# Hybrid decoder step on one core: the sums of w2's quarters made in SBUF and stored, or made in DRAM by copying and accumulating transfers

## The chip, the cores and the metric

The kernel runs on one core of a Trainium2 chip. The metric is the device time of one execution in microseconds (us), of which the median of several runs is taken. The engines are PE (matrix products; PEld is its weight load), DVE (vector), ACT (activations), POOL (general) and SP (which here only issues transfers). Transfers issued from SP, ACT and POOL go through three queues, which the profile calls q1 (SP), q10 (ACT) and q0 (POOL), to the same 16 DMA engines.

## The reference

The program computes one step of a one-layer decoder. 2048 prompt tokens and 8 x 8 sample tokens of width 1024 go through a common input projection. One half of the heads does forgetting attention (8 heads of 64, for the samples over 8192 cached positions), the other half an mLSTM recurrence. Then come the output projection, a layer norm, an MLP of width 4096 and a second layer norm.

```python
x1 = _layer_norm(DN_ALPHA * x + mix, ln1_g, ln1_b)
hid = jnp.square(jax.nn.relu(x1 @ w1))
return _layer_norm(DN_ALPHA * x1 + hid @ w2, ln2_g, ln2_b)
```

What matters here is `hid @ w2`. The kernel makes it by Strassen's scheme, seven products of half-sized blocks in place of eight, and for this it needs sums of w2's quarters.

## The kernel before, in words

The work runs in phases. Phase A makes the projections and the mLSTM. Phase B is the prompt's forgetting attention. Phase O makes the output projection and the first layer norm, phase C the MLP. The samples' attention over the cache is a generator whose steps are laid between the other work by a counter of estimated PE time (`tick`). In phase B that counter is set so that no step falls due; only six steps are called by hand, in units 10 to 15, each with one gather of cached keys on POOL (L1649). Every step runs inside `beside`, which holds its instructions behind the entries of the table `last` (the latest instruction of PE, ACT and DVE that the helpers have put there), each on its own engine.

**Phase B** (`phase_b`) runs over 64 units, 8 heads h by 8 groups g of 256 queries. Unit (h, g) reads 2g + 2 blocks of 128 keys, so late units of a head are longer than early ones. `scores` makes the score tiles of two blocks of 128 queries. For each of them POOL first makes `nd` (L938), the forget values `nl` of the diagonal block plus a causal mask; there are three buffers of it. PE writes q times k into a PSUM bank in two passes (L945, L946). DVE adds the forget values and keeps the maximum, for the blocks before the diagonal at L952 and for the diagonal block, with `nd`, at L956; this empties the bank for the next product. L959 makes the row's maximum. One unit later `values` takes the exponential on ACT (L973), the sums on DVE (L974), transposes the weights on PE (L986), copies them out on ACT (L989) or DVE (L991) and multiplies by v (L995). `finish`, twice per head, brings the reciprocal sums through DRAM (`drl`, L1016, L1019) and scales the output on POOL (L1021). SP loads the queries `qn` (L918), the keys `kn` (L900), and `nl` and `vn` (L894, L895).

**The sums of w2.** The host lays w2 out as 8 steps p by 4 quarters of 128 x 1024 (512 KB each). Strassen's scheme needs four sums for each step, kept in the DRAM tensor `dw2[p, j]`: j = 0 is quarters 0 + 1, j = 1 is 3 + 1, j = 2 is 0 + 1 + 3, j = 3 is 0 + 1 + 3 + 2 (each made from the one before in the same buffer). `w2_sum` is called 34 times, from unit 10 on, two calls in three units. Four calls make one step: ACT's queue loads quarters 0 and 3 into two SBUF buffers `wr` (L1094, 16 loads in all), POOL's queue adds other quarters to these buffers by accumulating transfers (L1097, 32) and stores the sums to `dw2` (L1100, 32). Each of these waits for the transfer before it on the same buffer, on the queue of the engine that issues it. POOL issues `nd` and the scaling of L1021 from the same stream of instructions, in order.

There are five `wr` buffers of 128 x 1024; phase O loads the output weights into them from unit 60 on (L1126).

**Phase C** makes the MLP in four blocks of tokens. In every block each step p loads quarters of w2 and the four sums of `dw2` by SP (L1137; 128 loads of `dw2` in all), splits them into a high and a low part (ACT at L154, DVE at L157) and makes three matmuls for each product (L162, L163, L164).

The order of instructions on each engine is laid down when the program is built, by a scheduler that simulates a timeline; `tc.issue_after(ins)` keeps an instruction behind `ins` on its engine.

Of the kernel before, what the change touches and what calls it, by code (L numbers as in the profile page):

```python
# [10 lines left out]
F32 = mybir.dt.float32  # L11
# [3 lines left out]
OP = mybir.AluOpType  # L15
# [37 lines left out]
def body(ctx, tc, I, O, stages):  # L53
    nc = tc.nc
    V, A, G, T, SY = nc.vector, nc.scalar, nc.gpsimd, nc.tensor, nc.sync
# [3 lines left out]
    drm = ctx.enter_context(tc.tile_pool(name="drm", bufs=1, space=DRAM))  # L59
# [11 lines left out]
    dR = drm.tile([NB, FH, PAST], F32, name="dR")  # L71
    dqb = drm.tile([2, NB, 32, 16 * 8], F32, name="dqb")
    dx1 = drm.tile([TOT, D], F32, name="dx1")
    dw2 = drm.tile([8, 4, 128, 1024], F32, name="dw2")

    ident = cst.tile([128, 128], F32, name="ident")
    nhalf = cst.tile([128, 8], F32, name="nhalf")
# [5 lines left out]
    def pad(pool, n):  # L83
        pads.append(n)
        V.memset(pool.tile([128, n // 4], F32, name=f"pad_{len(pads)}x")[:, 0:1], 0.0)
# [22 lines left out]
    last = {}  # L108
# [17 lines left out]
    def attend():  # L126

        r = beside(acc[1])
        if r == 3:
            acc[3] = acc[1]  # L130
        if r in (0, 3):
            acc[1] = None

    def tick(us):

        macc[0] += us
        while macc[1] and macc[0] > macc[2]:
            macc[0] -= macc[2]
            if beside(macc[1][0]) == 0:
                macc[1].pop(0)  # L140
        if not macc[1]:
            macc[0] = 0.0
        acc[0] += us
        while acc[1] is not None and acc[0] > acc[2]:
            acc[0] -= acc[2]
            attend()
# [718 lines left out]
    def phase_b():  # L865
# [8 lines left out]
        def bank():  # L874

            turn[0] += 1
            if turn[0] % 3 == 0:
                return pps.tile([128, 512], F32, name="pS", tag="sX", bufs=1)
            return ppb.tile([128, 512], F32, name="pS", bufs=2)

        def head(h):
            vn = Z[0]["vn"] if h == 0 else pb.tile([128, 16, 64], F32, name="vn", bufs=2)
            nl = pb.tile([128, 2048], F32, name="nl", bufs=2)
            if h == 0:
                masks.append(pb.tile([128, 128], F32, name="dmask"))
            ls = pb.tile([128, 32], F32, name="ls", bufs=2)
            ks = pb.tile([128, 2048], F32R, name="ks", bufs=2)
            G.memset(ls, 1.0)
            return dict(h=h, ls=ls, nl=nl, vn=vn, ks=ks)

        def forget_values(z, a, n):

            h = z["h"]
            SY.dma_start(z["nl"][:, a:a + n], dap(dnl, h * TOT + a, [[0, 128], [1, n]]))  # L894
            SY.dma_start(z["vn"][:, a // 128:(a + n) // 128], vp[a:a + n, h * 64:h * 64 + 64].rearrange("(t p) c -> p t c", p=128))  # L895
# [7 lines left out]
        def keys(z, g, kn=None):  # L903

            h = z["h"]
            kn = keys_load(h, g) if kn is None else kn
            if h == 0:
                forget_values(z, g * 512, 512)
            k = z["ks"][:, g * 512:(g + 1) * 512]
            split_hi(k, kn)  # L910
            split_lo(k[64:128], kn[64:128], k[64:128])

        def queries(z, g):

            h = z["h"]
            qn = pb.tile([128, 256], F32, name="qn", bufs=3)
            for d in range(2):
                SY.dma_start(qn[d * 64:d * 64 + 64], dq[h // 2, h % 2 * 64:h % 2 * 64 + 64, g * 256:(g + 1) * 256])  # L918
            qh = pb.tile([128, 256], F32R, name="qh", bufs=3)
            if h == 0 and g == 0:  # L920
                z["vn"] = pb.tile([128, 16, 64], F32, name="vn", bufs=2)
            ql = pb.tile([128, 256], F32R, name="ql", bufs=3)
            split_hi(qh, qn)
            split_lo(ql, qn, qh)
            z["q", g] = qh, ql

        def scores(z, g):

            qh, ql = z.pop(("q", g))
            nl, ks = z["nl"], z["ks"]  # L930
            out = []
            for i in range(2):
                qt = 2 * g + i
                n = (qt + 1) * 128
                qs = slice(i * 128, i * 128 + 128)
                mx = pb.tile([128, 8], F32, name="mx", bufs=6)
                nd = pb.tile([128, 128], F32, name="nd", bufs=3)
                G.tensor_tensor(nd, nl[:, qt * 128:n], dmask, op=OP.add)  # L938
                st = []
                j = 0  # L940
                for a in range(0, n, 512):
                    b = min(n, a + 512)
                    w = max(b - a, 256)
                    pS = bank()
                    T.matmul(pS[:, :w], qh[:, qs], ks[:, a:a + w], start=True, stop=False)  # L945
                    last["PE"] = T.matmul(pS[:, :w], ql[:, qs], ks[:, a:a + w], start=False, stop=True)  # L946
                    tick(0.42)
                    sp = pb.tile([128, 512], F32, name="S", bufs=10)
                    st.append(sp)
                    e = min(b, qt * 128)  # L950
                    if e > a:
                        last["DVE"] = V.tensor_tensor_reduce(out=sp[:, :e - a], in0=pS[:, :e - a], in1=nl[:, a:e], scale=1.0, scalar=NEG,  # L952
                                               op0=OP.add, op1=OP.max, accum_out=mx[:, j:j + 1])
                        j += 1
                    if b == n:
                        V.tensor_tensor_reduce(out=sp[:, e - a:b - a], in0=pS[:, e - a:b - a], in1=nd, scale=1.0, scalar=NEG,  # L956
                                               op0=OP.add, op1=OP.max, accum_out=mx[:, j:j + 1])
                        j += 1
                V.tensor_reduce(mx[:, 7:8], mx[:, :j], axis=AX.X, op=OP.max, negate=True)  # L959
                out.append((st, mx))  # L960
            return out
# [66 lines left out]
        kn = keys_load(0, 0)  # L1028
        queries(Z[0], 0)
        Z[0].update(head(0))  # L1030
        dmask = masks[0]
        pad(pb, 64)
        V.memset(dmask, 0.0)
        G.affine_select(dmask, dmask, pattern=[[-1, 128]], compare_op=OP.is_ge, fill=NEG, base=0, channel_multiplier=1)
        keys(Z[0], 0, kn)
        sc = {}
        LA = 1
        for n in range(len(units) + LA):
            if 10 <= n < 16 and acc[1] is not None:
                attend()  # L1040
            while len(w2_done) < 34 and n >= 10 + len(w2_done) * 3 // 2:
                w2_sum()
            if n == 60:
                wo.extend(half_wo(0, q) for q in range(4))
            if n < len(units):
                h, g = units[n]
                sc[n] = scores(Z[h], g)
                if h == 0 and g % 2 == 0 and g < 6:
                    keys(Z[0], g // 2 + 1)
                if h < 7:  # L1050
                    if g == 3:
                        Z[h + 1] = head(h + 1)
                        forget_values(Z[h + 1], 0, S)
                    if g >= 4:
                        keys(Z[h + 1], g - 4)
                if n + 1 < len(units):
                    queries(Z[units[n + 1][0]], units[n + 1][1])
            if n >= LA:
                h, g = units[n - LA]
                values(Z[h], g, sc.pop(n - LA))  # L1060
        es.close()
# [13 lines left out]
    def raw():  # L1075

        return pcw.tile([128, 1024], F32, name="wr", bufs=5)
# [2 lines left out]

        return pcw.tile([128, 1024], F32, name="xr", bufs=2)[:n]

    w2_done, w2_q = [], {}

    def w2_sum():

        k = len(w2_done)
        w2_done.append(k)

        def load(p):  # L1090
            for q in (0, 3):
                w2_q[p, q] = raw()
                with tc.issue_after(last["ACT"].ins):
                    A.dma_start(w2_q[p, q], I["w2"][p, q])  # L1094

        def add(p, a, q):
            G.dma_start(w2_q[p, a], I["w2"][p, q], accum_op=OP.add)  # L1097

        def store(p, a, j):
            G.dma_start(dw2[p, j], w2_q[p, a])  # L1100

        p, j = divmod(k, 4)
        if k == 0:
            load(0)
        if j == 0:
            if p:
                store(p - 1, 0, 2)
                add(p - 1, 0, 2)
            if p < 8:
                add(p, 0, 1)  # L1110
        elif j == 1:
            if p:
                store(p - 1, 0, 3)
            if p < 8:
                store(p, 0, 0)
                add(p, 3, 1)
        elif j == 2:
            store(p, 3, 1)
            add(p, 0, 3)
        elif p < 7:  # L1120
            load(p + 1)

    def half_wo(hf, q):

        r = raw().rearrange("p (k c) -> p k c", k=2)
        SY.dma_start(r, I["w_o2"][hf, q].rearrange("p (k c) -> p k c", k=2))  # L1126
        return r
# [800 lines left out]
```

## Time and profile before

| what | value |
|---|---|
| median of 3 runs | 3317.51 us (3309.04 to 3324.81) |
| the profiled execution's own time | 3327.42 us |
| its span | 3325.7 us |
| mean granted clock of PE | 0.976 |
| PE busy | 3155.1 us (95%) |
| DVE busy | 2106.5 us (63%) |
| ACT busy | 1504.9 us (45%) |
| POOL busy | 928.8 us (28%) |
| DMA, mean | 223 GB/s |
| phase B in the trace | about 928 to 1400 us |

The profile is one execution. A line such as L938 is the line of the kernel's code that made the instruction. An entry such as `[5.10 <-DMA wr<-w]` says that the engine stood idle for 5.10 us before the instruction and that a transfer from w2 into a `wr` buffer ended this. In the tables of stretches each engine has its busy us and, in brackets, its number of instructions; PEclk is the granted share of PE's full clock, and the DMA share is the mean busy share of the 16 DMA engines. POOL is named with the transfers that it issues, but the issue is not counted as a compute operation of the kernel; what it waits for before an issue holds all that is queued behind it on POOL.

### The profile page before, as it was taken

To read this page: it belongs to the slowest core of one execution; us is meant where nothing else is said; L and a number is where in the kernel's file an instruction comes from. 1 tells how busy PE (TensorE), PEld (TensorE's weight loads), DVE (VectorE), ACT (ScalarE), POOL (GpSimd) and SP (SyncE) were. 2 spreads that over 40 slices of the span, in tenths; PEclk is the share of its full clock that TensorE was granted. 3 is DMA by queue.
4 is the path that set the end of the run, shared out by engine and by line. 5 is a ranking of instruction groups with operands and counts; after the bars stand their busy time and mean duration, and the time that the engine had idled before them with its cause. 6 is when DMAs were issued, how large, how long until landed. Compare 5 with 4: busy or idle time off the path is not lost.

```text
span 3325.7 us, 58093 instructions
## 1 busy us (share of the span) xinstructions
PE 3155.1 (95%) x21681; PEld 2571.7 (77%) x21681; DVE 2106.5 (63%) x5079; ACT 1504.9 (45%) x2966; POOL 928.8 (28%) x977
## 2 busy tenths in 40 slices
PE   8999999998978989999999999999999999799997
PEld 8998998888945657677677777676777777698895
DVE  6857565455366868644465668656586666856658
ACT  4333343333267878722244454343454444444442
POOL 0031232332323334266533333423323121100000
PEclk9999999998988999999999999999999999999998
DMA  5575766766658777387787878878779766644333
GB/s 184 151 222 183 235 222 216 248 203 214 215 173 218 201 202 204 100 308 263 277 313 266 312 273 286 310 254 329 281 269 339 244 216 207 196 149 127 114 108 98
DMA packets 342002, 742.76 MB, mean 223 GB/s; under 512 B 63896, under 2 KB 177944, under 8 KB 340824
## 3 DMA queue, kind: packets, MB, share of 16 engines
q1 hardware_dynamic: 252856, 416.71, 39.7%
q0 software_dynamic: 83520, 304.12, 26.2%
q10 hardware_dynamic: 5344, 18.22, 1.6%
q8 instruction: 171, 2.80, 0.3%
q14 instruction: 111, 0.91, 0.1%
HBM read 669.32 MB, written 69.60 MB: 222 GB/s over the span
## 4 chain that ended last, share of the span: by engine, by line
PE 45%; DMA 4%; DVE 2%; issue 1%; POOL 1%; ACT 0%; DVEq 0%; POOLq 0%; ACTq 0%; SPq 0%
PE ph L162 8%; PE ph L163 7%; PE ph L164 7%; PE py L162 5%; PE py L164 5%; PE py L163 5%; PE sO L1784 3%; DMA vt<-cache_v,idxV 2%; PE sQ L1672 2%; DMA kT<-cache_k,idxK 1%; PE sT L1741 1%; DVE wl L157 1%; DVE y L1348 1%; DMA xr<-cache_v,idxV 0%; PE pw L163 0%
## 5 line engine op out<-in xcount | busy, mean ns | idle before, releaser
L157 DVE TENSOR_TENSOR wl<-wr,wh 128x1024 fp32r<-128x1024 f32 x364 | 445.8, 1226 | 375.8 <-ACT wh L154 372.1
L154 ACT ACTIVATE wh<-wr 128x1024 fp32r<-128x1024 f32 x364 | 382.8, 1054 | 329.3 <-PE ph L163 167.8
L162 PE MATMUL ph<-x1h,wh 128*128 128x512 f32 (+1 forms) x1280 | 455.9, 356 | 0.5 <-DVE x1l L157 0.5
L163 PE MATMUL ph<-x1l,wh 128*128 128x512 f32 (+1 forms) x1280 | 453.8, 355 | 0.0
L1649 POOL DMA_INDIRECT kT<-cache_k,idxK x256 | 273.3, 1068 | 643.2 <-PE sQ L1672 579.4
L164 PE MATMUL ph<-x1h,wl 128*128 128x512 f32 (+1 forms) x1280 | 451.2, 354 | 0.0
L162 PE MATMUL py<-wh,hh 128*128 128x512 f32 x896 | 357.2, 400 | 4.5 <-DVE y L1348 2.3
L163 PE MATMUL py<-wl,hh 128*128 128x512 f32 x896 | 352.1, 393 | 0.0
L164 PE MATMUL py<-wh,hl 128*128 128x512 f32 x896 | 350.7, 394 | 1.0 <-DVE hl L157 1.0
L1348 DVE TENSOR_TENSOR y<-y,py 128x512 f32<-128x512 f32 x416 | 280.5, 681 | 63.6 <-PE py L164 58.8
L162 PE MATMUL pm<-xh,whi 128*128 128x256 f32 (+1 forms) x1024 | 301.6, 295 | 0.0
L163 PE MATMUL pm<-xl,whi 128*128 128x256 f32 (+1 forms) x1024 | 297.2, 290 | 0.0
L164 PE MATMUL pm<-xh,wlo 128*128 128x256 f32 (+1 forms) x1024 | 296.1, 289 | 0.0
L1760 POOL DMA_INDIRECT vt<-cache_v,idxV x164 | 178.9, 1091 | 342.0 <-PE sO L1784 276.8
L162 PEld LDWEIGHTS ph<-x1h,wh 128*128 128x128 f32 x1280 | 241.4, 189 | 41.1 <-issue 7.4
L163 PEld LDWEIGHTS ph<-x1l,wh 128*128 128x128 f32 x1280 | 241.5, 189 | 33.9 <-issue 3.3
L164 PEld LDWEIGHTS ph<-x1h,wl 128*128 128x128 f32 x1280 | 241.0, 189 | 34.2 <-issue 3.7
L162 PE MATMUL pm<-whi,xh 128*128 128x256 f32 (+2 forms) x816 | 238.3, 292 | 8.5 <-ACT whi L154 7.9
L163 PE MATMUL pm<-wlo,xh 128*128 128x256 f32 (+2 forms) x816 | 233.8, 287 | 0.6 <-DVE wlo L157 0.6
L164 PE MATMUL pm<-whi,xl 128*128 128x256 f32 (+2 forms) x816 | 233.4, 286 | 0.0
L973 ACT ACTIVATE S<-S,mx 128x512 f32<-128x512 f32 (+2 forms) x320 | 207.8, 653 | 44.3 <-DVE mx L959 41.2
L162 PEld LDWEIGHTS py<-wh,hh 128*128 128x128 f32 x896 | 168.5, 189 | 53.1 <-issue 12.4
(371 smaller groups left out, 6845.4 us busy)
## 6 DMA issues: line engine op xcount, KB each, us to landing
wr<-w SPq DMA_DIRECT2D x224, 512.0 KB
wr<-dw SPq DMA_DIRECT2D x128, 512.0 KB
wra<-w_in SPq DMA_DIRECT2D x104, 512.0 KB
Rb<-dR SPq DMA_DIRECT2D x128, 128.0 KB
wr<-w POOLq DMA_DIRECT2D x32, 512.0 KB, 6.1
dw<-wr POOLq DMA_DIRECT2D x32, 512.0 KB, 4.2
xn<-xp_t SPq DMA_DIRECT2D x16, 512.0 KB
kn<-k_prompt SPq DMA_DIRECT2D x64, 128.0 KB
```

The costliest lines, as they stand in the source:

```text
L154: last["ACT"] = A.activation(dst, src, AF.Copy, scale=scale)
L157: r = (eng or V).tensor_tensor(dst, src, hi.bitcast(F32), op=OP.subtract)
L162: T.matmul(ps, wh, xh, start=first, stop=False, skip_group_check=shared)
L163: T.matmul(ps, wh, xl, start=False, stop=False, skip_group_check=shared)
L164: last["PE"] = T.matmul(ps, wl, xh, start=False, stop=stop, skip_group_check=shared)
L973: last["ACT"] = A.activation(sp[:, :w], sp[:, :w], AF.Exp, bias=mx[:, 7:8], accum_out=lp[:, k:k + 1])
L1348: V.tensor_tensor(y, y, ps, op=op)
L1649: G.indirect_dma_start(out=piece(n), out_offset=None, in_=ck, in_offset=IO(ap=idxK[:, b, j // 2, j % 2:j % 2 + 1], axis=0))
L1672: r = T.matmul(pq[h4 * 32:h4 * 32 + 32, hg].rearrange("p (k c) -> p k c", k=2), z["qb"][:, hd], kv, start=(db == 0), stop=(db == 1), skip_ ...
L1741: T.transpose(p[:, f], z["U"][u][:, hg, f].rearrange("p k t -> p (k t)"), ident)
L1760: G.indirect_dma_start(out=vt.rearrange("p f c -> p (f c)"), out_offset=None, in_=cv, in_offset=IO(ap=idxV[:, b, (kt % 4) * 4 + kt // 4, f ...
L1784: after_ = T.matmul(po[r:r + 32], z["PT"][:, hg, 2 * f + g, pg].rearrange("p h q -> p (h q)"), vts[f][:, g, hg * 256:(hg + 1) * 256], star ...
```

## The change

All sums are made by transfers from DRAM to DRAM, issued by POOL, without SBUF buffers and without loads from ACT. There are eight kinds in a list, each done for all eight steps p before the next kind begins: copy quarter 0 to `dw2[p, 0]`; copy quarter 3 to `dw2[p, 1]`; add quarter 1 to j = 0; add quarter 1 to j = 1; copy `dw2[p, 0]` to j = 2; add quarter 3 to j = 2; copy `dw2[p, 2]` to j = 3; add quarter 2 to j = 3. That is 64 transfers of 512 KB, 32 copying and 32 accumulating. They begin at unit 1. A running sum is raised in each unit by 64/150 times 1, 1, 2, 2, 3, 3, 4, 4 for g = 0 to 7, and as many transfers are issued as it has reached. Each is held behind the last `nd` (`last["POOL"]`, set at L938). Since `beside` reads the same table, the steps of the samples' generator are now held behind the last `nd` on POOL too. `dw2` gets rows of 1152 elements, of which 1024 are used.

```diff
-    dw2 = drm.tile([8, 4, 128, 1024], F32, name="dw2")
+    dw2 = drm.tile([8, 4, 128, 1152], F32, name="dw2")[:, :, :, 0:1024]
...
-                G.tensor_tensor(nd, nl[:, qt * 128:n], dmask, op=OP.add)
+                last["POOL"] = G.tensor_tensor(nd, nl[:, qt * 128:n], dmask, op=OP.add)
...
+        last.pop("POOL", None)
...
+        w2_due = [0.0]
...
-            while len(w2_done) < 34 and n >= 10 + len(w2_done) * 3 // 2:
+            w2_due[0] += 64 * (n % 8 // 2 + 1) / 150
+            while n and len(w2_done) < min(64, w2_due[0]):
                 w2_sum()
...
-    w2_done, w2_q = [], {}
+    W2_SUMS = ((0, I["w2"], 0, False), (1, I["w2"], 3, False), (0, I["w2"], 1, True), (1, I["w2"], 1, True),
+               (2, dw2, 0, False), (2, I["w2"], 3, True), (3, dw2, 2, False), (3, I["w2"], 2, True))
+    w2_done = []
...
         k = len(w2_done)
         w2_done.append(k)
-
-        def load(p):
-            for q in (0, 3):
-                w2_q[p, q] = raw()
-                with tc.issue_after(last["ACT"].ins):
-                    A.dma_start(w2_q[p, q], I["w2"][p, q])
-
-        def add(p, a, q):
-            G.dma_start(w2_q[p, a], I["w2"][p, q], accum_op=OP.add)
-
-        def store(p, a, j):
-            G.dma_start(dw2[p, j], w2_q[p, a])
-
-        p, j = divmod(k, 4)
...
+        j, src, q, more = W2_SUMS[k // 8]
+        with tc.issue_after(last["POOL"].ins):
+            G.dma_start(dw2[k % 8, j], src[k % 8, q], **({"accum_op": OP.add} if more else {}))
```

More of the change, by code (lines that the diff above doesn't have):

```diff
@@ L1088, in w2_sum @@
         w2_done.append(k)
-        def load(p):
-            for q in (0, 3):
-                w2_q[p, q] = raw()
-                with tc.issue_after(last["ACT"].ins):
-                    A.dma_start(w2_q[p, q], I["w2"][p, q])
-        def add(p, a, q):
-            G.dma_start(w2_q[p, a], I["w2"][p, q], accum_op=OP.add)
-        def store(p, a, j):
-            G.dma_start(dw2[p, j], w2_q[p, a])
-        p, j = divmod(k, 4)
[L1103 to L1121, printed above, removed]
+        j, src, q, more = W2_SUMS[k // 8]
+        with tc.issue_after(last["POOL"].ins):
+            G.dma_start(dw2[k % 8, j], src[k % 8, q], **({"accum_op": OP.add} if more else {}))
     def half_wo(hf, q):
```

## The prediction

> **What bounds the kernel now.** I read the page first, then a table of stretches of the prompt's attention, then the waits in it, then one stretch in order of time.
>
> ```profile
> span 3325.7 us, 58093 instructions
> ```
>
> The profiled execution took 3327.42 us, 1.7 us more than its span. The median of the runs shown is 3317.51 us (3309.04 to 3324.81), so this execution lies 0.3% above it; I work out a difference on the profiled execution and take it off the median.
>
> The stretches. Columns: the stretch, its length, busy us and instructions of PE, PEld, DVE, ACT, POOL, then PEclk, DMA share, GB/s.
>
> ```profile
> 928.00:1400.00 472.00, 431.11 (x2877) 299.78 (x2876) 350.37 (x1375) 364.78 (x1023) 152.26 (x229) 0.95 0.67 179
> 1000.00:1335.00 335.00, 309.77 (x2080) 216.42 (x2076) 252.49 (x985) 262.19 (x737) 123.82 (x184) 0.95 0.78 204
> 1048.00:1061.00 13.00, 4.29 (x15) 2.43 (x14) 3.56 (x14) 5.40 (x17) 2.67 (x5) 0.59 0.70 186
> 1061.00:1078.00 17.00, 16.58 (x96) 11.81 (x97) 14.34 (x62) 11.55 (x32) 5.18 (x11) 0.81 0.63 188
> 1100.00:1150.00 50.00, 49.62 (x348) 34.56 (x345) 41.23 (x163) 44.17 (x126) 17.79 (x27) 1.00 0.79 206
> 1168.00:1184.00 16.00, 6.32 (x29) 4.91 (x28) 4.15 (x20) 5.54 (x16) 3.79 (x8) 0.77 0.78 236
> 1184.00:1198.00 14.00, 14.00 (x89) 9.46 (x87) 11.65 (x53) 9.99 (x29) 4.98 (x9) 0.89 0.66 151
> 1335.00:1380.00 45.00, 45.00 (x318) 32.35 (x318) 35.75 (x151) 38.38 (x110) 11.81 (x19) 1.00 0.27 82
> 1400.00:3325.00 1925.00, 1852.94 (x11350) 1453.12 (x11350) 1218.30 (x2123) 809.68 (x1244) 539.38 (x480) 0.98 0.69 241
> ```
>
> The prompt's attention fills 928 to 1400. PE bounds it: 49.62 of 50 us in 1100 to 1150, at 348/50 = 6.96 matmuls per us. But in two holes (1048 to 1061, 1168 to 1184) PE is busy 4.29 of 13 and 6.32 of 16 us, and in the stretches behind them it is busy at a granted clock of 0.81 and 0.89. Between 1000 and 1335, where the sums of w2 run, 25.2 us of PE are idle; in 1335 to 1380, without them, none.
>
> Who waited, 990 to 1350 (total us, times, longest):
>
> ```profile
> POOL dw L1100 <- DMA wr<-w: 93.2, 27, 6.3
> POOL wr L1097 <- DMA dw<-wr: 35.3, 14, 6.4
> ...
> DVE S L956 <- POOL nd L938: 25.8, 5, 8.4
> ...
> PE pS L945 <- DVE mx L956: 14.0, 6, 7.0
> ...
> POOL ot L1021 <- DMA rl<-drl: 12.1, 5, 4.5
> ...
> PE pS L945 <- DVE mx L959: 8.1, 3, 7.7
> ```
>
> POOL stands 93.2 + 35.3 = 128 us waiting for w2's own transfers to land. Its other task, nd (nl plus the mask of the diagonal block, L938), is queued behind. Mostly that costs nothing, since nd has three buffers; five times it came too late (25.8 us of DVE), and PE waited 14.0 + 8.1 = 22.1 us for DVE at the next product. The longest of these, in order of time:
>
> ```profile
> 1053.36 0.88 POOL L1097 DMA_DIRECT2D wr<-w  x1 [6.08 <-DMA dw<-wr]
> 1053.96 0.76 POOL L938 TENSOR_TENSOR nd<-nl,dmask 128x128 f32<-128x128 f32 x1
> 1054.75 0.29 DVE L956 CUSTOM_DVE_ANT_0 S<-pS,nd 128x128 f32<-128x128 f32 x1 [8.42 <-POOL nd L938]
> ...
> 1055.20 0.76 PE L945 MATMUL pS<-ks,qh 128*128 128x512 f32 x1 [7.05 <-DVE mx L956]
> ```
>
> POOL waits 6.08 us for a store to land, then comes nd, then DVE after 8.42 us idle, then PE after 7.05 us idle, because the PSUM bank is drained only once nd is there.
>
> **The change, part by part.** *The waits go.* Today one pair of SBUF buffers carries a step of w2: load, accumulate, store, accumulate, store, each waiting for the one just issued. In the new order each kind of sum is made for all 8 steps before the next kind, so a transfer's forerunner was issued 8 or 16 transfers earlier. The price on the path, by matmuls at the clean 6.96 per us: 1048 to 1061 did 15 (2.2 us of work), so 10.8 us are lost; 1061 to 1078 did 96 (13.8), 3.2 lost; 1168 to 1184 did 29 (4.2), 11.8 lost; 1184 to 1198 did 89 (12.8), 1.2 lost. Together 27.0. Smaller holes are left out of the sum. Bound from above: all 2080 matmuls of 1000 to 1335 at 6.96 per us take 298.9 us, so 36 us. What is late next: PE itself, as in 1335 to 1380, where it is busy 45.00 of 45 with ACT at 38.38.
>
> *Six gathers move.* The diff also enters POOL in `last`, and `beside` holds every step of the samples' generator behind all entries of `last`. So the six key gathers that the code calls at units 10 to 15 can no longer be issued ahead of the phase's first nd. Today they are, at its very start. The queues from 915 to 945, then PE's holes and the longest wait of ACT there:
>
> ```profile
> q1 hardware_dynamic: 5664, 4.39, 53.5%
> q0 software_dynamic: 864, 3.15, 32.5%
> ```
>
> ```profile
> 926.87 0.80 PE L945 MATMUL pS<-ks,qh 128*128 128x256 f32 x2 [7.84 <-ACT qh L154]
> ...
> 938.32 1.18 PE L986 MATMUL pt<-ident,S 128*128 128x128 f32 x3 [10.19 <-ACT S L973]
> ```
>
> ```profile
> ACT ks L154 <- DMA kn<-k_prompt: 8.9, 1, 8.9
> ```
>
> PE stands 18 us while the first qn and kn come in over engines that are 53.5 + 32.5 = 86% busy, and the gathers take 0.325 x 30 = 9.8 us of all engines there. Without them the first keys land up to 9.8 us sooner; at the least nothing, if the loads' own chain sets the time. I take 5 us off, the middle. In units 10 to 15 the gathers add the same 9.8 us to w2's traffic, far ahead of their use in phase O.
>
> *What is issued.* The instructions, as they are now:
>
> ```profile
> L1097 POOL DMA_DIRECT2D wr<-w x32: 877/902/1550, 1000.0 to 1327.3; - x32
> ...
> DMA to landing us min/median/max: 5.4/6.1/9.5
> ```
>
> ```profile
> L1100 POOL DMA_DIRECT2D dw<-wr x32: 549/583/897, 1006.1 to 1333.7; - x32
> ...
> DMA to landing us min/median/max: 2.9/4.2/9.4
> ```
>
> POOL issues 64 transfers before and after. A transfer between two DRAM tensors is in no row; its issue lies between 0.55 (shortest store) and 1.55 us (longest accumulate). I take 0.9, the accumulates' median: 58 us for now 32 x 0.902 + 32 x 0.583 = 48. POOL is busy 152 of 472 us, and 0.9 us ahead of an nd is covered by its three buffers; at 1.55 us it would be so too. If that cover went, 64 x 0.9 = 58 us would be at stake. ACT loses 16 issues and their waits; it is busy 365 of 472 us and off the path, so nothing.
>
> *The new wait.* An accumulate, or a copy out of dw2, waits on POOL for the transfer 8 or 16 places back, with nd and the scaling of ot (L1021) queued behind it. Before, w2 starts at unit 10; now it starts at unit 1 (about 938) and the pacing reaches 64 at unit 60, now about 1335 and 28 us earlier after: some 370 us, 5.8 us per transfer, so 8 places are 46 us against the longest landing of 9.5. Cost nothing, as long as the DMA engines keep up.
>
> *Whether they do.* The queues from 990 to 1345 (packets, MB, share of 16 engines):
>
> ```profile
> q0 software_dynamic: 9216, 33.56, 39.7%
> q1 hardware_dynamic: 29921, 30.35, 29.7%
> q10 hardware_dynamic: 2304, 8.39, 7.5%
> ```
>
> w2 holds q0 and q10. q0: 0.397 x 355 = 141 us of all engines for 64 transfers, 4.4 for an accumulate with its store. q10: 27 us for 16 loads, 1.66 each. A new pair (one copy, one accumulate) costs no less than 4.4, if the DRAM legs hide; no more than 4.4 + 2 x 1.66 = 7.7, if each of the two pays a DRAM leg like a load on top. I take 5.5, nearer to the row of the transfers that POOL issues now. 32 pairs: 141, 246, and 176 us. SP's queue adds 0.297 x 370 = 110 us. So the share is (176 + 110)/370 = 77%, where 1100 to 1150 runs PE at 49.62 of 50 with 0.79; the upper end gives 96%. A figure of the Trainium skill, "DMA: Bandwidth & Descriptors", "Latency and other measured facts": copies between two HBM tensors with a padded row pitch ran at 214 GB/s; by that, as an estimate, a copy of 512 KB takes 2.45 us, and with 4.4 for the accumulate a pair takes 6.9, or 89%. No row here shows such a copy.
>
> *Earlier start and pitch.* Eight or nine transfers now fall into head 0 (928 to 990). I give 2 us for that, between 0 and 9 (one more wait like that for kn), and 2 us for scaling waits like the 12.1 us of ot, which now stand alone (0 to 4.5, the longest). dw2's rows lie 4608 bytes apart instead of 4096 and are still read 4 KB at a time in phase C: nothing, at a DMA share of 0.69 there; were each of the 128 loads half as dear again (0.8 us), 106 us of DMA time would be spread over 1925 us.
>
> **Sum:** -27 - 5 + 2 + 2 = -28 us: 3327.4 becomes 3299.4 in the profile, and the median 3317.5 becomes **3289.5 us** (-0.8%).
>
> **Rivals.** *1. The DMA engines become the bound (slower).* Place: the accumulates, kinds 3, 4, 6 and 8 of the eight. If a pair costs more than (370 - 110)/32 = 8.1 us, transfers pile up, the one 8 places back hasn't landed, and POOL stands before nd again. From (398 - 110)/32 = 9.0 us the gain is gone, from 9.5 us on it is slower by 0.5%; at 10 us, 320 + 110 = 430 us are needed where 370 are there, +60, 3350 us. Against it: my upper end from rows is 7.7. For it: a DRAM destination has to be read as well, and nothing here shows that. The same page and section of the Trainium skill gives HBM access as 0.2 us on average and 2 us at high load. By the second figure, as an estimate, 8 rows one after another on an engine make 16 us per accumulate, 512 us in all, 622 with the 110 of SP where 370 are there, and the time would be about 3540 us. Against this stands a row: a load of now, 9 packets per engine (2304/16/16), holds the engines 1.66 us, 0.2 us a row, so reads overlap. Chance 0.10.
>
> *2. The gain is given back to late loads (within 0.5%).* SP's kn, qn and nl share the engines with w2 from unit 1 on. With two or three waits as long as a median landing (6.1 us) in head 0 and at the heads' starts, and no gain at the start, 17 to 23 us return: 3306 to 3312. For it: a share of 77 to 96%. Against it: the stretch with 0.79. Chance 0.20.
>
> *3. The waits don't go (slower).* If the order is kept for all of dw2 rather than for each block of 512 KB, each transfer waits for the one before: 63 x about 6 = 380 us of POOL waiting, three times the 128, which cost 27; at that rate 81, so 3371 us. Against it: all 32 stores go to dw2, and none of the long waits before L1100 names another store. Chance 0.04.
>
> **How the numbers follow.** 0.5% is 16.6 us, about what a measurement of this kernel can tell from no change. Forecast (faster) 0.66, rival 2 (same) 0.20, rivals 1 and 3 (slower) 0.14. The range goes from 3268 (3317.5 less both bounds, 36 + 9.8, and some 4 us for the median's own scatter) to 3330 (all given back at the upper end of the DMA's cost, and 12 us of scatter); that leaves out the slower rivals and little else.
>
> **What would show it.** Right: POOL's waits for w2's transfers near nothing; no "DVE S L956 <- POOL nd L938"; no hole of several us in the attention, granted clock near 1.00 from 960 on; q10 gone there; the six gathers issued after 980, PE's holes at 918 to 938 shorter by some 5 us; the attention ends some 28 us sooner and all behind it is as long as before. Wrong: q0's share far above 50% of the attention, landings beyond 20 us, POOL waiting before transfers of dw2, or waits named kn, qn or nl.

## The result, and the profile after

The changed kernel takes 3286.56 us (median of 6 runs, 3274.42 to 3290.92) against 3317.63 us for the kernel before beside it: a ratio of 0.9903, 95% interval 0.9874 to 0.9931. A second set of the same kernel gave 3285.58 against 3320.9, ratio 0.9896 (0.9878 to 0.9914). The forecast was 3289.5. The profiled execution took 3288.1 us, its span is 3286.4 us.

The page of the changed kernel, its first lines:

```profile
span 3286.4 us, 58046 instructions
...
PE 3148.6 (96%) x21681; PEld 2564.4 (78%) x21681; DVE 2099.1 (64%) x5079; ACT 1500.7 (46%) x2966; POOL 912.9 (28%) x977
```

PE has as many instructions and nearly the same busy time as before (3155.1 us); what went is idle time. One stretch of the changed kernel (length, busy us of PE, PEld, DVE, ACT, POOL, then granted clock, DMA share, GB/s):

```profile
1000.00:1335.00 335.00, 331.98 (x2292) 232.20 (x2292) 275.88 (x1093) 286.59 (x812) 120.92 (x187) 1.00 0.67 167
```

In 1000 to 1335 PE is now busy 331.98 of 335 us with 2292 matmuls at a granted clock of 1.00, where it was 309.77 with 2080 at 0.95. POOL's waits from 990 to 1350, the whole list down to its end:

```profile
POOL nd L938 <- DVE mx L956: 80.3, 36, 6.6
POOL ot L1021 <- DMA rl<-drl: 65.2, 12, 9.9
POOL nd L938 <- DVE ls L974: 39.1, 16, 5.3
POOL ot L1021 <- ACT PT L989: 9.7, 1, 9.7
POOL ot L1021 <- ACT ot L1001: 8.5, 1, 8.5
POOL ot L1021 <- issue: 7.5, 1, 7.5
POOL nd L938 <- DVE mx L959: 4.9, 8, 1.0
POOL ot L1021 <- ACT S L973: 2.9, 1, 2.9
POOL kT L1624 <- issue: 0.8, 5, 0.2
POOL dw L1096 <- issue: 0.3, 1, 0.3
```

Not one wait for a transfer of w2 to land is left. In the kernel before, the two rows shown held 128 us, and a third, `POOL wr L1097 <- DMA wr<-w`, another 20.5: 149 us in all. nd now waits for DVE, which reads its buffers (mx L956, ls L974); so POOL is ahead of DVE, not behind it. The scaling of ot now waits 65.2 us for rl; PE does not feel it.

The gathers have moved, as read from the diff. POOL of the changed kernel, in order of time:

```profile
986.79 1.07 POOL L1624 DMA_INDIRECT kT<-cache_k,idxK  x1 [0.16 <-issue]
987.87 0.58 POOL L1096 DMA_DIRECT2D dw<-w  x1
988.46 0.88 POOL L938 TENSOR_TENSOR nd<-nl,dmask 128x128 f32<-128x128 f32 x1
```

The first gather goes out at 986.79 instead of about 918, just ahead of a transfer of w2 and of nd, and neither of these waits for it. And PE's holes at the start of the attention:

```profile
927.68 0.79 PE L945 MATMUL pS<-ks,qh 128*128 128x256 f32 x2 [4.00 <-ACT qh L154]
932.12 1.18 PE L986 MATMUL pt<-ident,S 128*128 128x128 f32 x3 [3.19 <-ACT S L973]
```

They were 7.84 and 10.19 us.

To compare kernels I cut each profiled execution at three marks of PE's rows: the last start of the mLSTM's last transposes (L609), the first transpose of the attention's weights (L986), and the first matmul of the output projection (pw). "Ahead" is the time up to the first mark, "start" from the first mark to the second, "attention" from the second to the third, "rest" from there to the span's end. Before: 938.3 - 918.6 = 19.7, 1401.5 - 938.3 = 463.2, 3325.7 - 1401.5 = 1924.2. The ratio is that of the timed runs, with its interval, each against the kernel before run beside it (medians 3316.8 to 3320.9).

| kernel | ahead | start | attention | rest | median us | ratio to before |
|---|---|---|---|---|---|---|
| before | 918.6 | 19.7 | 463.2 | 1924.2 | 3317.6 | 1 |
| changed | 923.3 | 8.8 | 434.9 | 1919.4 | 3286.6 | 0.9903 (0.9874 to 0.9931) |
| changed, second set | 911.8 | 9.0 | 438.8 | 1923.4 | 3285.6 | 0.9896 (0.9878 to 0.9914) |
| gathers_only | 923.2 | 9.9 | 457.2 | 1922.3 | 3310.2 | 0.9965 (0.9951 to 0.9980) |
| sums_only | 919.4 | 19.3 | 440.3 | 1925.0 | 3306.2 | 0.9957 (0.9942 to 0.9972) |
| by_step | 915.3 | 8.8 | 443.3 | 1929.3 | 3292.6 | 0.9908 (0.9886 to 0.9929) |
| by_step_again | 923.7 | 9.1 | 439.5 | 1924.7 | 3293.9 | 0.9908 (0.9889 to 0.9928) |
| from_head1 | 924.1 | 10.0 | 445.8 | 1919.2 | 3294.8 | 0.9918 (0.9902 to 0.9935) |
| no_sums | 916.4 | 9.2 | 437.4 | 1924.3 | 3289.0 | 0.9916 (0.9883 to 0.9949) |
| nd_on_dve | 917.4 | 11.5 | 450.0 | 1921.5 | 3301.8 | 0.9943 (0.9927 to 0.9960) |
| sbuf_pairs | 915.4 | 19.0 | 465.6 | 1918.2 | 3327.3 | 1.0026 (1.0006 to 1.0047) |
| double | 918.8 | 9.5 | 522.2 | 1926.8 | 3370.7 | 1.0154 (1.0120 to 1.0188) |

From before to changed the start gives 10.9 us and the attention 28.3 us. The rest differs by 4.8 us between these two executions, and by as much between executions of kernels that don't differ there (by_step 1929.3 and 1924.7); the dw2 rows with a pitch of 4608 bytes, read in that part, cost nothing that shows. The time ahead of the first mark, in which no edit changes the work, takes 4.7 us longer in the changed kernel's trace, and in all these traces it lies between 911.8 and 924.1. So a difference of a few us between the spans of two traces says little; start and attention are what to compare.

### The profile page after: what moved, and what is told of

The parts are those of the page before. It is cut to its first block, busy times and chain, and to the rows that moved or that the text cites. A ratio compares the mean times of both kernels' runs of the same rounds, so it can differ in the third digit from the quotient of the medians.

```text
span 3286.4 us, 58046 instructions
## 1 busy us (share of the span) xinstructions
PE 3148.6 (96%) x21681; PEld 2564.4 (78%) x21681; DVE 2099.1 (64%) x5079; ACT 1500.7 (46%) x2966; POOL 912.9 (28%) x977
## 4 chain that ended last, share of the span: by engine, by line
PE 45%; DVE 3%; DMA 3%; issue 1%; POOL 1%; ACT 1%; another core or an unknown queue 0%; DVEq 0%; POOLq 0%; ACTq 0%; SPq 0%
PE ph L162 7%; PE ph L163 7%; PE ph L164 7%; PE py L162 6%; PE py L164 5%; PE py L163 5%; PE sO L1759 3%; PE sQ L1647 2%; DMA vt<-cache_v,idxV 1%; DVE wl L157 1%; PE sT L1716 1%; DVE y L1323 1%; DMA kT<-cache_k,idxK 0%; PE pw L163 0%; PE pw L164 0%
```

## The experiments

**gathers_only: one half of the change alone.** The kernel before, with POOL entered in `last`:

```diff
-                G.tensor_tensor(nd, nl[:, qt * 128:n], dmask, op=OP.add)
+                last["POOL"] = G.tensor_tensor(nd, nl[:, qt * 128:n], dmask, op=OP.add)
```

> The kernel before, with POOL entered in the table that holds the samples' steps back, and nothing else: w2's sums stay in SBUF with their waits. Theory (two separate gains): the six gathers go out in units 10 to 15, PE's first transposes of the attention come about 11 us earlier after the end of the mLSTM (19.7 us before, 8.8 us in the changed kernel), the holes behind POOL's waits for w2 stay (about 27 us), and the time falls by 5 to 11 us to about 3307 to 3313 us. Rival (the changed kernel's gain is one, POOL's waits; the earlier start is a side effect of w2's loads having gone): the start stays at about 19 us and the time at 3317 us.

Measured: 3310.15 us, ratio 0.9965, so some 12 us less (7 to 16), 8.6 by the medians. The start fell from 19.7 to 9.9 us. The holes in the attention stayed, and they show more than the profile of before did. PE, then ACT and POOL of gathers_only:

```profile
1021.93 2.56 PE L986 MATMUL pt<-ident,S 128*128 128x128 f32 x9 [6.60 <-ACT PT L989]
1167.13 0.55 PE L945 MATMUL pS<-ks,qh 128*128 128x256 f32 x1 [6.61 <-DVE mx L959]
```

```profile
1020.92 0.33 ACTq L1094 DMA_DIRECT2D wr<-w  x1
1021.29 0.58 ACT L989 COPY PT<-pt 128x512 f32<-128x512 f32 x1 [8.54 <-DMA rl<-drl]
```

```profile
1157.59 0.54 POOL L1100 DMA_DIRECT2D dw<-wr  x1 [1.89 <-DMA wr<-w]
1165.28 0.89 POOL L1097 DMA_DIRECT2D wr<-w  x1 [7.15 <-DMA dw<-wr]
1165.87 1.19 POOL L938 TENSOR_TENSOR nd<-nl,dmask 128x128 f32<-128x128 f32 x2
```

The hole at 1167 is the known one: POOL stands 7.15 us before an accumulate whose buffer is still being stored, and nd comes after it. The hole at 1021 is another: ACT stands 8.54 us, and the first thing that it does then is to issue one of w2's loads (L1094), which waits for its buffer; the copy of the transposes, for which PE waits, is queued behind it. The row names rl as the releaser; that is the transfer that landed last by the profile, and a load into wr does not need it. By the code the load needs the store of its buffer; the trace does not show when that store landed.

**sums_only: the other half alone.** The changed kernel, with nd kept in a variable of its own and not in `last`:

```diff
-                last["POOL"] = G.tensor_tensor(nd, nl[:, qt * 128:n], dmask, op=OP.add)
+                last_nd[0] = G.tensor_tensor(nd, nl[:, qt * 128:n], dmask, op=OP.add)
...
-        with tc.issue_after(last["POOL"].ins):
+        with tc.issue_after(last_nd[0].ins):
```

> The changed kernel, but POOL is kept out of that table, so that the six gathers can go out at the start of the attention as before. Theory: no hole behind a wait for w2, POOL's waits for transfers of w2 near 0, the stretch from the first transposes to the output projection as in the changed kernel (435 us against 463 us before), but the start slow again (about 19 us); time 3317 less 28, about 3289 to 3297 us, that is 5 to 11 us above the changed kernel's 3286.6. Rival: nothing but the waits counts, then the time is that of the changed kernel, 3286 us.

Measured: 3306.2 us, ratio 0.9957, some 14 us less than before (9 to 19). The start is back at 19.3 us, with the same two holes, and the attention is 440.3 us. PE at the start of sums_only:

```profile
928.07 0.79 PE L945 MATMUL pS<-ks,qh 128*128 128x256 f32 x2 [8.24 <-ACT qh L154]
938.73 1.18 PE L986 MATMUL pt<-ident,S 128*128 128x128 f32 x3 [9.40 <-ACT S L973]
```

So there are two separate gains, and the rival that only the waits count falls. But the time lies 9 us above the range that I had expected (3289 to 3297): in timed runs the sums alone save about half of the 28 us, although the attention in the trace is nearly as short as the changed kernel's. The two halves add up to 26 us, each uncertain by 5; together they measured 32 and 35.

**by_step and by_step_again: the same transfers in another order.**

```diff
-        j, src, q, more = W2_SUMS[k // 8]
+        j, src, q, more = W2_SUMS[k % 8]
...
-            G.dma_start(dw2[k % 8, j], src[k % 8, q], ...
+            G.dma_start(dw2[k // 8, j], src[k // 8, q], ...
```

> The changed kernel with the same 64 transfers from DRAM to DRAM in the other order: all eight kinds of one step, then the next step, so that an adding or copying transfer waits for the one issued one or two places before it. Theory (the distance between a transfer and its forerunner is what takes the waits away): POOL's waits for w2's transfers come back, some 50 to 150 us in total, nd is late again, PE stands for several us some times, 10 to 30 us slower than the changed kernel, 3297 to 3317 us. Rival (the DRAM route by itself, or the SBUF buffers and ACT's loads saved by it, makes the gain): within 5 us of 3286 us, whatever POOL waits.

Measured: 3292.59 us, ratio 0.9908, under my theory's range and 6 us from the changed kernel, just outside the rival's 5. My theory fell in its main part: the waits came back and cost next to nothing. POOL's waits for w2 in by_step_again, 905 to 1390:

```profile
POOL dw L1096 <- DMA dw<-w: 41.8, 13, 5.2
...
POOL dw L1096 <- DMA dw<-dw: 30.8, 9, 4.9
```

That is 72.6 us in 22 waits, none longer than 5.2, and DVE waits for nd once, 1.6 us. The three buffers of nd cover a wait of 5 us if nothing of that length came just before. In the kernel before, several transfers stood between one nd and the next, so the waits added up. POOL there, ahead of the long wait that the prediction shows:

```profile
1040.80 0.80 POOL L938 TENSOR_TENSOR nd<-nl,dmask 128x128 f32<-128x128 f32 x1
1046.70 0.58 POOL L1100 DMA_DIRECT2D dw<-wr  x1 [5.10 <-DMA wr<-w]
```

With the 6.08 us of the next wait, 12.4 us pass from the end of this nd to the next at 1053.96. Ahead of the hole at 1168 to 1184 it is 14.6 us, ahead of the one of gathers_only at 1167 15.6 us. I ran the order by steps again beside the changed kernel:

> The order step by step, which measured 3292.6 us with 68 us of POOL's waits for w2 and no hole behind nd. Theory as it stands after that run (waits up to 5 us at a time are covered by the three buffers of nd; what cost time before were waits in twos, 5 and 6 us, without room between): the same time as the changed kernel within 5 us. Rival (the distance of 8 transfers matters): 5 to 15 us slower than the changed kernel beside it.

Measured: 3293.92 us and 0.9908 (0.9889 to 0.9928), the changed kernel 3285.58 and 0.9896 (0.9878 to 0.9914). The medians lie 8 us apart, in the rival's range and not in my theory's; the intervals overlap over most of their length, and the attention took 439.5 us against 438.8. Whether the order kind by kind is worth a few us stays open; it is not what makes the 28 us. What keeps the waits short and apart in by_step is not separated either: against the kernel before it has the route through DRAM, each transfer held behind the last nd, and a start at unit 1 with a slower pace.

**nd_on_dve: nothing of the scores behind POOL's waits.** The kernel before, with nd made by DVE:

```diff
-                G.tensor_tensor(nd, nl[:, qt * 128:n], dmask, op=OP.add)
+                V.tensor_tensor(nd, nl[:, qt * 128:n], dmask, op=OP.add)
```

> The kernel before with one change: nd is made by DVE instead of POOL, so that nothing of the scores stands behind POOL's waits for w2; sums in SBUF, loads on ACT and gathers at the start as before. DVE gets 128 more instructions of 128 x 128, some 0.2 us each, 26 us more on an engine that is busy 350 of 472 us. Theory (nd behind POOL's waits is the price of the sums): POOL waits as long as before or longer, the holes of PE behind nd are gone, the stretch from the first transposes to the output projection falls from 463 us to 440 to 450, 8 to 20 us faster than before, 3297 to 3309 us. Rival (w2's loads on ACT's queue cost as much, or DVE becomes late): within 6 us of 3317 us, with PE's holes behind ACT.

Measured: 3301.79 us, ratio 0.9943, 19 us less than before (13 to 24). POOL's waits for w2 in nd_on_dve, 990 to 1350, and the stretch beside them:

```profile
POOL dw L1100 <- DMA wr<-w: 110.2, 26, 8.9
POOL wr L1097 <- DMA wr<-w: 42.8, 11, 14.3
POOL wr L1097 <- DMA dw<-wr: 35.7, 11, 5.9
```

```profile
1000.00:1335.00 335.00, 322.36 (x2220) 223.77 (x2217) 289.19 (x1160) 276.39 (x788) 79.49 (x94) 1.00 0.80 210
```

POOL waits longer than before, 188.7 us against 149 in the same three rows, and PE has no hole of 2 us left in that stretch; the granted clock is 1.00 and PE busy 322.36 against 309.77. This shows that it was nd behind these waits that cost PE its time, and not the waits themselves. It does not reach the 331.98 of the changed kernel; DVE does 128 instructions more (0.376 us each in the mean by the trace, 0.28 in the median, more than I had put down).

The start fell to 11.5 us although the gathers still go out at 917; two holes of 2.33 and 2.18 us follow it. The loads hardly came sooner there. What changed is the order of ACT's instructions. ACT of the kernel before, then of nd_on_dve:

```profile
935.72 0.63 ACT L154 ACTIVATE ks<-kn 128x512 fp32r<-128x512 f32 x1 [8.90 <-DMA kn<-k_prompt]
937.77 0.40 ACT L973 ACTIVATE S<-S,mx 128x128 f32<-128x128 f32 x1 [1.42 <-DVE mx L959]
```

```profile
928.35 0.40 ACT L973 ACTIVATE S<-S,mx 128x128 f32<-128x128 f32 x1 [4.11 <-DVE mx L959]
...
933.69 0.63 ACT L154 ACTIVATE ks<-kn 128x512 fp32r<-128x512 f32 x1 [4.01 <-DMA kn<-k_prompt]
```

In the kernel before, the split of the second keys stands ahead of the first exponential and waits for kn; in nd_on_dve the exponential goes first. Counted from the first mark, that split starts after 17.1 us before, 16.3 in nd_on_dve, and 8.8 in gathers_only. So only holding the gathers back brings the keys sooner, and by these rows some 8 of the 19 us here come from ACT's order and not from nd behind POOL's waits.

**sbuf_pairs: four buffers in SBUF, two steps of w2 side by side.** The calls of `w2_sum` were written anew for pairs of steps:

```diff
+        if j == 0:
+            add(p, 0, 1), add(p + 1, 0, 1)
+        elif j == 1:
+            add(p, 3, 1), add(p + 1, 3, 1)
+        elif j == 2:
+            store(p, 0, 0), store(p + 1, 0, 0)
...
```

> The kernel before, sums in SBUF and gathers at the start, but with four buffers instead of two: two steps of w2 side by side, so that a transfer waits for one that was issued one or two calls (two to four transfers) before and never for the one just issued. Theory (only the distance counts, not the DRAM route): POOL's waits for w2 fall from 149 us to under 75 us, at most one or two holes behind nd, 10 to 25 us faster than before, 3293 to 3307 us. Rival (SBUF buffers tie loads on ACT and stores together, so the waits only move): within 8 us of 3317 us.

Measured: 3327.27 us, ratio 1.0026, a little slower than before and outside both ranges. It did not do what I meant: POOL's waits for w2 from 990 to 1350 are 92.5 + 21.6 + 13.4 = 128 us against 149 in the same three rows of before, because in three of eight calls the two transfers wait for the two of the call just before:

```profile
POOL dw L1099 <- DMA wr<-w: 92.5, 31, 7.5
...
POOL wr L1096 <- DMA wr<-w: 21.6, 9, 4.8
POOL wr L1096 <- DMA dw<-wr: 13.4, 10, 6.5
```

POOL and PE at the longest:

```profile
1056.97 0.56 POOL L1099 DMA_DIRECT2D dw<-wr  x1 [7.51 <-DMA wr<-w]
1057.55 1.48 POOL L938 TENSOR_TENSOR nd<-nl,dmask 128x128 f32<-128x128 f32 x3
```

```profile
1058.49 0.55 PE L945 MATMUL pS<-ks,qh 128*128 128x256 f32 x1 [7.06 <-DVE mx L956]
```

It is the same hole again, so this run speaks for nd behind long waits, but says nothing on whether SBUF sums with few waits would have done as well. That stays open.

**no_sums: the floor.** The changed kernel without the loop that calls `w2_sum`, the MLP reading quarter 1 of w2 for every sum.

> The changed kernel without any of the 64 transfers; the MLP then loads quarter 1 of w2 where it would load a sum, so the sums are left out of the computation and all loads of the MLP are as many and as large as before. It is the floor: what the 64 transfers still cost. Theory (they are hidden but for their issue): 0 to 5 us faster than the changed kernel, 3281 to 3287 us, PE busy 99% of the stretch 1000 to 1330 in both. Rival (the DMA engines' share still delays loads): 10 us or more faster, below 3277 us.

Measured: 3289.01 us, ratio 0.9916 (0.9883 to 0.9949), the same as the changed kernel as far as the intervals tell. The stretch of no_sums:

```profile
1000.00:1335.00 335.00, 330.58 (x2283) 231.15 (x2282) 272.56 (x1086) 286.18 (x808) 89.27 (x138) 1.00 0.29 86
```

Without the transfers the DMA share is 0.29 instead of 0.67 and POOL is busy 32 us less, but PE does 2283 matmuls there against 2292. The 64 transfers of the changed kernel are free within what these runs can tell.

**from_head1: w2 starts at unit 8.**

```diff
-            w2_due[0] += 64 * (n % 8 // 2 + 1) / 150
+            w2_due[0] += 64 * (n % 8 // 2 + 1) / 130 if n >= 8 else 0
```

> The changed kernel with w2's transfers starting at unit 8 instead of unit 1 and a little denser pacing (64/130 instead of 64/150), so that they end at the same unit. Theory (SP's first loads are delayed by w2's transfers in head 0 by a few us): the holes of 4.0 and 3.2 us at the start of the attention and the short waits for kn and qn shrink, 2 to 5 us faster than the changed kernel, 3282 to 3285 us. Rival (those loads are late for their own reasons): the time of the changed kernel within 1 us, as far as 5 rounds can tell.

Measured: 3294.82 us, ratio 0.9918, outside both expectations: no gain, by the medians 8 us above the changed kernel. The start is 10.0 us with holes of 3.98 and 4.47. The first loads are not late for w2's sake; in the changed kernel its first transfer is issued at 929.98, when the first of the two holes is already over. The attention took 445.8 us; whether the denser pacing costs something or this is one execution's scatter, the intervals don't say.

**double: every transfer twice.**

```diff
-            G.dma_start(dw2[k % 8, j], src[k % 8, q], ...
+            for d in (dw2, dw3):
+                G.dma_start(d[k % 8, j], (d if src is dw2 else src)[k % 8, q], ...
```

> The changed kernel with each of the 64 transfers made twice, the second time into another DRAM tensor that nothing reads: 128 transfers, 64 of them accumulating. It asks how near the DMA engines are to being the bound. By the changed kernel's rows (q0 39.0% and q1 33.3% of 375 us) q0 would take about 75% and both queues some 110% of the attention's first 375 us. Theory (the DMA engines have a margin of about a quarter, then they bound): transfers pile up, POOL waits for w2 again, loads of qn and kn come late, 20 to 60 us slower than the changed kernel, 3305 to 3345 us. Rival (room enough, packets of the queues overlap): under 8 us slower, below 3295 us.

Measured: 3370.66 us, ratio 1.0154, by the medians 54 us slower than before and 84 slower than the changed kernel. The queues in 935 to 1310, then waits from 928 to 1440:

```profile
q0 software_dynamic: 14942, 54.39, 56.0%
q1 hardware_dynamic: 30952, 31.35, 28.4%
```

```profile
POOL ot L1022 <- DMA rl<-drl: 91.4, 11, 19.4
...
ACT ot L1002 <- DMA dmix<-ot: 46.4, 4, 18.7
...
ACT qh L155 <- DMA qn<-dq: 27.9, 7, 6.5
```

The time lies beyond the upper end that I had expected, and the place is another: POOL waits only 0.4 us for a landing of w2. What comes late are SP's transfers (rl by up to 19.4 us, the store of ot by up to 18.7, qn by up to 6.5). The way from there to PE shows at the longest wait for rl. SP, then POOL, ACT and PE:

```profile
1154.46 13.17 SPq L919 DMA_DIRECT2D qn<-dq  x1
1167.72 1.19 SPq L1020 DMA_DIRECT2D rl<-drl  x2
```

```profile
1172.78 1.25 POOL L1022 TENSOR_TENSOR ot<-ot,rl 64x512 f32<-64x512 f32 x1 [19.40 <-DMA rl<-drl]
1184.60 0.36 ACT L1002 COPY ot<-po 64x256 f32<-64x256 f32 x1 [13.19 <-DMA dmix<-ot]
1185.50 1.12 PE L987 MATMUL pt<-ident,S 128*128 128x128 f32 x4 [12.40 <-ACT PT L990]
```

SP spends 13.17 us on one issue of qn, and rl, next in its order, goes out only at 1167.72. So ot is scaled and stored late, ACT waits for its buffer, and PE behind ACT for 12.40 us. DVE never waits for nd here. The share of 56.0 + 28.4 = 84% is a mean: of 40 equal slices of this stretch 25 are at 90% or more (15 in the changed kernel). By the cost per pair worked out below, the doubled transfers and SP's queue would need 398 us where the prediction has 370. So the run shows the engines overloaded; it does not show that 84% is the limit.

## Why the prediction was right

**The mechanism** was right in its main step, nd queued behind POOL's waits for w2, and all signs that the prediction named are there: no wait for w2, no hole behind nd, granted clock 1.00, q10 gone, gathers after 980. The time was 3286.6 and 3285.6 against 3289.5. One step of it is not needed for most of the gain: by_step keeps waits for the transfer one or two places back and is 6 and 8 us from the changed kernel. That the total came out within 4 us is partly luck, as the terms show.

**The waits** were put at 27.0 us, and the two profiled executions differ in the attention by 28.3. Alone, though, this half gives 14 us by the timed runs (9 to 19), and taking nd out from behind the waits gives 19, some 8 of it at the start, where ACT's order had changed; in the trace its attention is 13.2 us shorter. The profiled execution of before was slower than its median, and gathers_only, with the same sums, took 457.2 us for the attention, not 463.2. I had priced the holes of one execution; they differ from execution to execution in number and place.

**The gathers** were put at 5 us, between 0 and 9.8. The start fell by 9.7 to 10.9 us in every kernel that holds the gathers back; alone they gave 12 (7 to 16). This is the term that I sized too small: I took the middle for want of a reason, and the upper end, all of the DMA time that the gathers take there, was near what came. The two errors, this one and the waits, have opposite signs by the timed runs, and the sum came out near because of that.

**The two give-backs** of 2 us do not show. For the first, from_head1 keeps w2 out of head 0 and is no faster. In the 60 us from the first transposes PE is idle 6.1 us in the changed kernel and 4.6 in from_head1, but 6.5 in no_sums, which has none of the transfers; a cost of 2 us is within that scatter. The second did appear as a wait, 65.2 us of ot instead of 12.1, but no wait of PE in the attention follows from it.

**ACT** I put at nothing. gathers_only shows a hole of 6.60 us of PE behind one of w2's loads on ACT, so this was wrong as a rule; in the profile of before the like was 2.24 us and left out.

**The DMA engines.** I took 5.5 us for a pair, between 4.4 and 7.7. The queue that carries w2 in two stretches of the changed kernel, 1215 to 1260 with copies only and 1260 to 1312 with accumulates only:

```profile
q0 software_dynamic: 989, 3.59, 26.9%
```

```profile
q0 software_dynamic: 1211, 4.44, 43.9%
```

At 144 packets for each transfer (9216 for 64 before) that is 6.9 copies in 0.269 x 45 = 12.1 us, 1.76 each, and 8.4 accumulates in 0.439 x 52 = 22.8 us, 2.71 each: 4.5 us for a pair, nearly the lower bound; the stretches cut some transfers at their edges. The figure of the Trainium skill's "DMA: Bandwidth & Descriptors" ("Latency and other measured facts") gave an estimate of 2.45 us for a copy; the trace has 1.76. The 2 us of HBM access at high load that the same section of the Trainium skill states do not show as a cost of each row: at one row after another an accumulate would have taken 16 us, and it takes 2.71. q0 and q1 together took 39.0 + 33.3 = 72% of 935 to 1310, where I had 77%.

**The rivals.** The third, an order kept for all of dw2, is excluded by the list of POOL's waits. The first did not come, since a pair costs 4.5 us and not 8.1 or more. double shows what an overload looks like: SP's transfers come late first (the second rival's mechanism), and POOL's waits for w2, the place that the first rival named, stay near nothing. At the changed kernel's 72% neither shows.

What stays open: whether the order by kinds is worth a few us against the order by steps; whether sums in SBUF with few waits would have done as well; why the sums alone save less in timed runs than the traces suggest. dw2 without the pitch wasn't tried.

## What to carry to other kernels

A wait on an engine that works in order costs what stands behind it, once it is longer than the buffers between. Here 72.6 us of waits, none over 5.2 us, made no hole; waits that kept POOL from the next nd for 12 to 16 us, or one of 7.51 us, did. Moving the victim to another engine showed it without touching the waits. Read a diff for what its small edits do elsewhere: one new entry in a table of latest instructions moved six gathers by some 70 us, and that was a third of the gain. Price holes from more than one execution when there are only a handful of them.

## What the runs showed of the hardware

A transfer from DRAM to DRAM held the DMA engines hardly longer than the like transfers with an end in SBUF: 1.76 us for a copy of 512 KB (a load of before 1.66), 4.5 for a copy and an accumulate (4.4 for an accumulate and a store before). With every transfer of w2 made twice (a mean DMA share of 84%), one issue on SP's queue lasted 13.17 us and what stood behind it came late, while POOL, whose queue carried the heavy load, waited 0.4 us in all for its own landings.
